# Rotary embedding on one core: the first batch's output stored in four quarters, one of them from SyncE's queue

## The chip, the cores and the metric

The kernel runs on one core of a Trainium2 chip. The metric is the device time of one execution in microseconds (us). The kernel before the change takes 163.11 us, the median of three runs (163.11 to 163.17).

## The reference

The input `x` is 8 batches of 2048 positions, 8 heads and 64 numbers, all float32 (33.5 MB); `cos` and `sin` are tables of 2048 x 32. The output has the size of `x`.

```python
x1 = x[..., :32]
x2 = x[..., 32:]
out1 = x1 * cos - x2 * sin
out2 = x1 * sin + x2 * cos
return concatenate([out1, out2], axis=-1)
```

Every number of `x` is read once and every number of the output is written once.

## The kernel before

**Tiling.** One batch is one tile of 128 partitions. A partition holds R = 16 consecutive positions of 512 numbers each, so a partition's row of a batch is 32 KB, and a batch is 4 MB. Five tiles `xts` (NBUF = 5) are used in turn: batch b lies in tile b % 5, the result is written over the input in place, and it is stored from there. So batch 5 can only be loaded when batch 0 has been stored, batch 6 when batch 1 has, and batch 7 when batch 2 has.

**Loads.** `load(b)` (lines 112 to 125) issues from SyncE's queue (SP). Batch 0 comes in three parts of 4, 4 and 8 positions (rows of 8, 8 and 16 KB in each partition), every other batch in one DMA with rows of 32 KB. Batches 0 to 4 are issued at the start (lines 135 to 137), one behind the other. For b of 5 and more, `load` first waits on SP for all stores of batch b - 5.

**Stores.** `store(b, lo, n, needs)` (lines 127 to 132) stores positions lo to lo + n of batch b. It waits on the issuing engine for the work that makes them. It issues from ScalarE's queue (ACT), except that the last batch is stored from SP. The list `FIRST` (line 269) cuts batch 0 into stores of 4, 4 and 8 positions, `LAST` cuts batch 7 into 7, 5, 3 and 1; the other batches are stored whole.

**Queues in the profile.** DMAs issued by SP are the DMA queue q1, those by ACT are q10. Both run on the same 16 DMA engines. A DMA over 128 partitions gives each DMA engine eight rows.

**Compute.** `PLANS` (lines 259 to 268) splits each batch into pieces. A piece of kind A (`on_vector`) takes one multiply on GpSimd (POOL, line 198, with the swapped halves and the sine), one multiply with the cosine (line 202) and one addition (line 221) on VectorE (DVE). Pieces B and C (`on_tensor`) leave the addition to TensorE (PE, lines 249 and 250), and ScalarE copies the sum back (line 253). Batch 0 is four A pieces of four positions. Its four additions end one after the other, and the loop behind each piece (lines 283 to 289) issues a store as soon as its positions are done. Every engine works in the order in which the loop over the batches emits the instructions.

Of the kernel before, what the change touches and what calls it, by code (L numbers as in the profile page):

```python
# [10 lines left out]
def kernel(  # L11
# [7 lines left out]
    nc = tc.nc  # L19
# [11 lines left out]
    NBUF = 5  # L31
    C = 512
    last = B - 1
# [44 lines left out]
    def wait(engine, point):  # L78
        engine.wait_ge(point[0].sem, point[1])  # L79
        mine = known.setdefault(engine, {})  # L80
        for count, v in [point, *told.get(point, {}).items()]:
            mine[count] = max(v, mine.get(count, 0))
# [10 lines left out]
    def need(engine, *points):  # L93
        for count, v in points:
            if v > known.get(engine, {}).get(count, 0):
                wait(engine, (count, v))
# [15 lines left out]
    def load(b):  # L112
        parts = [(0, 4), (4, 4), (8, 8)] if b == 0 else [(0, R)]
        if b >= NBUF:
            for point in stored[b - NBUF]:
                wait(nc.sync, point)
        for lo, n in parts:
            cols = slice(lo * HD, (lo + n) * HD)
            ins = nc.sync.dma_start(out=xts[b % NBUF][:, cols], in_=xv[b, :, cols])
            point = Count(f"ld{b}_{lo}").by(ins, nc.sync, 16)  # L120
            for r in range(lo, lo + n):
                landed[(b, r)] = point
            if b == 0 and lo == 0:
                cos_in = Count("cos_in").by(nc.sync.dma_start(out=cos_sb, in_=cos_src), nc.sync, 16)
        return cos_in if b == 0 else None

    def store(b, lo, n, needs):
        engine = nc.sync if b == last else nc.scalar
        need(engine, *needs)
        cols = slice(lo * HD, (lo + n) * HD)  # L130
        ins = engine.dma_start(out=ov[b, :, cols], in_=xts[b % NBUF][:, cols])
        stored.setdefault(b, []).append(Count(f"st{b}_{lo}").by(ins, engine, 16))

    sin_in = Count("sin_in").by(nc.scalar.dma_start(out=sin_sb, in_=sin_src), nc.scalar, 16)
    cos_in = load(0)
    for b in range(1, NBUF):
        load(b)

    need(nc.gpsimd, prod.by(nc.gpsimd.memset(eye, 0.0), nc.gpsimd))  # L139
    eye_done = prod.by(  # L140
# [71 lines left out]
    def on_vector(b, lo, n):  # L212

        nonlocal t1_read, turn
        pair = pairs[turn]
        turn = (turn + 1) % len(pairs)
        at, done = sines(b, lo, n, pair, 0)
        need(nc.vector, t1_read, landed[(b, lo)])
        wait(nc.vector, pair.by(times(t1[:, : n * HD], cos_ps, b, lo, n), nc.vector))
        t1_read = dve.by(  # L220
            nc.vector.tensor_add(out=region(b, lo, n), in0=t1[:, : n * HD], in1=products(at, n)),  # L221
            nc.vector,
        )
        read[at : at + n] = [t1_read] * n
        return t1_read

    def on_tensor(b, lo, n, crossed=False):


        nonlocal copied  # L230
        if crossed:
            at, before = place(n, n // 2)
            need(nc.vector, landed[(b, lo)], *before, sin_done)
            need(nc.vector, dve.by(times(products(at, n), sin_ps, b, lo, n), nc.vector))
        else:
            at, made = sines(b, lo, n, prod, n // 2)
            need(nc.vector, made)
        wait(nc.tensor, dve.by(times(region(b, lo, n), cos_ps, b, lo, n), nc.vector))
        xt, prods = region(b, lo, n), products(at, n)
        if crossed:  # L240
            xu, tu = (a.rearrange("p (g u d) -> p g u d", u=2, d=Dh) for a in (xt, prods))
            groups = [slice(j * 2 * H, (j + 1) * 2 * H) for j in range(n // 2)]
            work = [(xu[:, g, u], tu[:, g, 1 - u], eye if u else neye) for g in groups for u in range(2)]
        else:
            cols = [slice(j * HD, (j + 1) * HD) for j in range(n)]
            work = [(xt[:, c], prods[:, c], eye) for c in cols]
        for xj, tj, sign in work:
            wait(nc.tensor, copied)
            nc.tensor.matmul(o, eye, xj, start=True, stop=False)  # L249
            summed = mm.by(nc.tensor.matmul(o, sign, tj, start=False, stop=True), nc.tensor)  # L250
            wait(nc.scalar, summed)
            src = o.rearrange("p (g d) -> p g d", d=Dh) if crossed else o
            copied = act.by(nc.scalar.copy(xj, src), nc.scalar)  # L253
            read[at : at + n] = [summed] * n
        return copied
# [10 lines left out]
        "B1 A5 A5 A5",  # L266
        "B2 A5 A5 A4",
    )
    FIRST = [(0, 4), (4, 4), (8, 8)]
    LAST = [(0, 7), (7, 5), (12, 3), (15, 1)]  # L270
    wait(nc.tensor, eye_done)
    for b in range(B):
        plan, lo = [], 0
        for tile_ in PLANS[b].split():
            plan.append((tile_[0], lo, int(tile_[1])))
            lo += int(tile_[1])
        shares = {0: FIRST, last: LAST}.get(b, [(0, R)])
        done = {}
        for kind, lo, n in plan:
            point = on_vector(b, lo, n) if kind == "A" else on_tensor(b, lo, n, kind == "C")  # L280
            for r in range(lo, lo + n):
                done[r] = point
            while shares and all(r in done for r in range(shares[0][0], sum(shares[0]))):
                s0, sn = shares.pop(0)
                needs = {}
                for r in range(s0, s0 + sn):
                    count, v = done[r]
                    needs[count] = max(v, needs.get(count, 0))
                store(b, s0, sn, needs.items())
        if b + NBUF <= last:  # L290
            load(b + NBUF)
    for b in range(last + 1 - NBUF, last - 1):
# [49 lines left out]
```

## Time and profile before

| | |
|---|---|
| Median of three runs | 163.11 us |
| Time of the profiled execution | 163.16 us |
| Its span, from the first instruction to the last | 161.4 us |
| DVE busy | 140.3 us (87%) |
| POOL busy | 131.1 us (81%) |
| PE busy | 49.8 us (31%) |
| Bytes moved by DMA | 67.66 MB, mean 419 GB/s |
| Last addition on DVE, start and length | 150.91 us, 2.29 us |

The span is 1.8 us shorter than the time of the same execution; these 1.8 us lie before the first and behind the last instruction of the program. All places in time below count from the start of the span. For a queue the profile gives its packets, the bytes, and the time of its packets as a share of the 16 DMA engines' span. The time "to landing" of a DMA runs from its issue to its last semaphore update, so it includes the time in which it stood behind other DMAs.

### The profile page before, as it was taken

To read this page: it belongs to the slowest core of one execution; us is meant where nothing else is said; L and a number is where in the kernel's file an instruction comes from. 1 tells how busy PE (TensorE), PEld (TensorE's weight loads), DVE (VectorE), ACT (ScalarE), POOL (GpSimd) and SP (SyncE) were. 2 spreads that over 40 slices of the span, in tenths; PEclk is the share of its full clock that TensorE was granted. 3 is DMA by queue.
4 is the path that set the end of the run, shared out by engine and by line. 5 is a ranking of instruction groups with operands and counts; after the bars stand their busy time and mean duration, and the time that the engine had idled before them with its cause. 6 is when DMAs were issued, how large, how long until landed. Compare 5 with 4: busy or idle time off the path is not lost.

```text
span 161.4 us, 412 instructions
## 1 busy us (share of the span) xinstructions
PE 49.8 (31%) x76; PEld 16.3 (10%) x76; DVE 140.3 (87%) x55; ACT 14.8 (9%) x25; POOL 131.1 (81%) x35
## 2 busy tenths in 40 slices
PE   0000000048686400068886811830072001840000
PEld 0000000022222100022221301200020001210000
DVE  0069999999999999999999999799999999799900
ACT  3320000001212100001112110110001000110000
POOL 1399996996999989942995599999999999999100
PEclk9999999999999975555579995796555555597555
DMA  5999998998998999999999999999999999998996
GB/s 154 427 455 418 431 487 357 455 487 357 479 431 325 455 496 414 390 496 414 390 496 414 390 496 414 390 496 414 390 496 414 390 496 414 390 487 375 435 406 252
DMA packets 3603, 67.66 MB, mean 419 GB/s; under 512 B 400, under 2 KB 400, under 8 KB 912
## 3 DMA queue, kind: packets, MB, share of 16 engines
q1 hardware_dynamic: 2160, 38.01, 55.5%
q10 hardware_dynamic: 1440, 29.62, 42.7%
q14 instruction: 3, 0.02, 0.0%
HBM read 34.08 MB, written 33.55 MB: 419 GB/s over the span
## 4 chain that ended last, share of the span: by engine, by line
DVE 51%; POOL 35%; issue 5%; DMA 4%; POOLq 0%; ACTq 0%; SPq 0%
POOL t L198 32%; DVE t L202 24%; DVE xt L221 23%; DVE xt L202 5%; DMA sin_sb<-in_sin_dram 4%; POOL t L184 3%; POOLq L79 0%; ACTq L337 0%; SPq L85 0%
## 5 line engine op out<-in xcount | busy, mean ns | idle before, releaser
L198 POOL TENSOR_TENSOR t<-xt,sgn 128x2560 f32<-128x2560 f32 (+3 forms) x27 | 125.8, 4688 | 12.9 <-DVE xt L221 4.5
L202 DVE TENSOR_TENSOR t<-xt,cos_ps 128x2560 f32<-128x2560 f32 (+1 forms) x23 | 61.8, 2687 | 8.3 <-ACT cos_ps L156 7.7
L221 DVE TENSOR_TENSOR xt<-t,t 128x2560 f32<-128x2560 f32 (+1 forms) x23 | 61.8, 2685 | 4.6 <-POOL t L198 2.7
L249 PE MATMUL o<-xt,eye 128*128 128x512 f32 x38 | 27.9, 825 | 93.1 <-DVE xt L202 83.5
L253 ACT COPY xt<-o 128x512 f32<-128x512 f32 x19 | 11.1, 585 | 123.4 <-PE o L250 123.4
L249 PEld LDWEIGHTS o<-xt,eye 128*128 128x128 f32 x38 | 7.1, 233 | 112.8 <-DVE xt L202 53.1
L250 PE MATMUL o<-t,eye 128*128 128x512 f32 x26 | 16.5, 722 | 0.0
L202 DVE TENSOR_TENSOR xt<-xt,cos_ps 128x512 f32<-128x512 f32 (+2 forms) x7 | 11.2, 1594 | 0.1
L250 PE MATMUL o<-t,neye 128*128 128x512 f32 x12 | 8.8, 826 | 0.0
L250 PEld LDWEIGHTS o<-t,eye 128*128 128x128 f32 x26 | 6.1, 235 | 8.4 <-issue 8.4
L202 DVE TENSOR_TENSOR t<-xt,sin_ps 128x3072 f32<-128x3072 f32 x2 | 6.7, 3344 | 0.0
L184 POOL TENSOR_TENSOR t<-xt,sin_sb 128x1024 f32<-128x1024 f32 x1 | 2.3, 2347 | 5.0 <-DMA sin_sb<-in_sin_dram 5.0
L250 PEld LDWEIGHTS o<-t,neye 128*128 128x128 f32 x12 | 3.2, 264 | 4.5 <-issue 4.5
L184 POOL TENSOR_TENSOR t<-xt,sgn 128x1024 f32<-128x1024 f32 x1 | 2.3, 2323 | 0.0
L153 ACT ACT_TABLE_LOAD x1 | 1.3, 1283 | 1.3 <-SPq L85 1.3
L153 ACT ACTIVATE sgn<-sin_sb 128x512 f32<-128x512 f32 x1 | 0.6, 629 | 4.0 <-DMA sin_sb<-in_sin_dram 4.0
L139 POOL MEMSET eye<- 128x128 f32 x1 | 0.2, 204 | 0.5 <-SPq L85 0.5
L157 ACT COPY sgn<-sin_sb 128x512 f32<-128x512 f32 x1 | 0.6, 608 | 0.0
L156 ACT COPY cos_ps<-cos_sb 128x512 f32<-128x512 f32 x1 | 0.6, 580 | 0.0
L158 ACT COPY sin_ps<-sin_sb 128x512 f32<-128x512 f32 x1 | 0.6, 580 | 0.0
L141 POOL TENSOR_SCALAR_AFFINE_SELECT eye<-eye 128x128 f32<-128x128 f32 x1 | 0.3, 293 | 0.2 <-POOL eye L139 0.2
L161 ACT ACTIVATE neye<-eye 128x128 f32<-128x128 f32 x1 | 0.3, 307 | 0.0
(4 smaller groups left out, 0.4 us busy)
## 6 DMA issues: line engine op xcount, KB each, us to landing
xt<-in_x_dram SPq DMA_DIRECT2D x7, 4096.0 KB, 33.9
out_dram<-xt ACTq DMA_DIRECT2D x6, 4096.0 KB, 23.4
xt<-in_x_dram SPq DMA_DIRECT2D x2, 1024.0 KB, 6.5
xt<-in_x_dram SPq DMA_DIRECT2D x1, 2048.0 KB, 12.1
out_dram<-xt ACTq DMA_DIRECT2D x2, 1024.0 KB, 19.0
out_dram<-xt ACTq DMA_DIRECT2D x1, 2048.0 KB, 28.5
out_dram<-xt SPq DMA_DIRECT2D x1, 1792.0 KB, 11.4
out_dram<-xt SPq DMA_DIRECT2D x1, 1280.0 KB, 9.4
```

What stands on the lines that cost most here:

```text
L141: nc.gpsimd.affine_select(out=eye, in_=eye, compare_op=mybir.AluOpType.not_equal, fill=1.0, base=0, pattern=[[-1, P]], channel_multiplier=1,),
L153: nsin_done = act.by(nc.scalar.mul(sgn[:, :, 0, :], sin_sb, -1.0), nc.scalar)
L156: cos_done = act.by(nc.scalar.copy(cos_ps, cos_sb), nc.scalar)
L157: sgn_done = act.by(nc.scalar.copy(sgn[:, :, 1, :], sin_sb), nc.scalar)
L158: sin_done = act.by(nc.scalar.copy(sin_ps, sin_sb), nc.scalar)
L184: nc.gpsimd.tensor_mul(out=tu[:, :, u, :].rearrange("p (r h) d -> p r h d", h=H), in0=xu[:, :, 1 - u, :].rearrange("p (r h) d -> p r h d", ...
L198: ins = nc.gpsimd.tensor_mul(out=out, in0=swapped, in1=repeat(sgn[:, lo : lo + n], H))
L202: return nc.vector.tensor_mul(out=out.rearrange("p (r k d) -> p r k d", r=n, d=Dh), in0=region(b, lo, n).rearrange("p (r k d) -> p r k d", ...
L221: nc.vector.tensor_add(out=region(b, lo, n), in0=t1[:, : n * HD], in1=products(at, n)),
L249: nc.tensor.matmul(o, eye, xj, start=True, stop=False)
L250: summed = mm.by(nc.tensor.matmul(o, sign, tj, start=False, stop=True), nc.tensor)
L253: copied = act.by(nc.scalar.copy(xj, src), nc.scalar)
```

## The change

Batch 0 is stored in four DMAs of four positions each, all with rows of 8 KB, where before there were two of 8 KB rows and one of 16 KB rows. The second of the four (positions 4 to 7) is issued from SP and not from ACT. The loads of batches 3 and 4 are no longer issued at the start: they are issued on SP right behind this store, so SP's queue holds the loads of batches 0, 1 and 2, then the store, then the loads of batches 3 and 4. What the other engines run, and in which order, is as before.

```diff
     def store(b, lo, n, needs):
-        engine = nc.sync if b == last else nc.scalar
+        engine = nc.sync if b == last or (b, lo) == (0, 4) else nc.scalar
...
     cos_in = load(0)
-    for b in range(1, NBUF):
-        load(b)
+    load(1)
+    load(2)
...
-    FIRST = [(0, 4), (4, 4), (8, 8)]
+    FIRST = [(0, 4), (4, 4), (8, 4), (12, 4)]
...
                 store(b, s0, sn, needs.items())
+                if (b, s0) == (0, 4):
+                    load(3)
+                    load(4)
```

## The prediction

> **What bounds the kernel now.** I read the page's slices and its queues first. In the slices of about 4 us the digits of DVE and of the DMA engines are 8 or 9 nearly throughout, so there are two candidates.
>
> ```profile
> DVE  0069999999999999999999999799999999799900
> ...
> DMA  5999998998998999999999999999999999998996
> ...
> q1 hardware_dynamic: 2160, 38.01, 55.5%
> q10 hardware_dynamic: 1440, 29.62, 42.7%
> ```
>
> The queues' shares add up to 98.2% of 161.4 us, or 158.5 us of work on each of the 16 DMA engines. The trace's packet records show all 16 occupied from 2.5 to 159.8 us with no gap. Next I looked at the end: the timeline of the last stores and the last addition.
>
> ```profile
> 143.56 10.76 SPq L131 DMA_DIRECT2D out_dram<-xt  x4
> ...
> 150.91 2.29 DVE L221 TENSOR_TENSOR xt<-t,t 128x2048 f32<-128x2048 f32 x1
> ```
>
> DVE's last addition ends at 153.20 us and the last store is issued at 153.60, but the landings run on to 160.5 us. What DVE releases last is 768 + 256 KB, which at the queues' 432 GB/s is 2.4 us. The other 4 us or so are stores that were released earlier and still stand in line. The chain of waits names DVE and POOL because it follows semaphores; it does not see a DMA standing behind another. So the DMA engines set the end, and compute has a few microseconds of slack there. The time can only change if the DMA engines get more or less work, if they run dry somewhere, or if compute slips by more than its slack.
>
> **How the queues share an engine.** These are issues and landings of single DMAs: the load of batch 2 (issued 3.38), the load of batch 4 (4.40) and the second store of batch 0 (18.35).
>
> ```profile
> xt<-in_x_dram SPq DMA_DIRECT2D x1, 4096.0 KB, 34.7
> ```
>
> ```profile
> xt<-in_x_dram SPq DMA_DIRECT2D x1, 4096.0 KB, 66.3
> ```
>
> ```profile
> out_dram<-xt ACTq DMA_DIRECT2D x1, 1024.0 KB, 22.7
> ```
>
> The loads run in the order of issue: batch 2 lands at 38.1 us, batch 3 at 52.5, batch 4 at 70.7. The store of 1 MB lands at 41.1 us, so it takes 12 us from the first store's landing (29.0). In the packet records each engine alternates between the queues row by row: 1.213 us for a load row of 32 KB, 0.309 us for a store row of 8 KB. Eight such pairs are 12.2 us, as seen. A store row of 16 KB takes 0.611 us.
>
> **Part 1, smaller rows.** The half with 128 rows of 16 KB becomes 256 rows of 8 KB: 2 x 0.309 - 0.611 = 0.007 us for each, times eight rows per engine, is +0.06 us. One more DMA adds one completion packet of 0.009 us per engine. Does a DMA more cost anything besides? Not where DMAs queue: the last two stores (768 and 256 KB, issued one behind the other) land 0.65 us apart, no more than the 0.67 us of eight rows of 2 KB (0.084 us each).
>
> **Part 2, SP waits for DVE.** SP now holds the loads of batches 3 and 4 until the second addition ends, at 18.3 us instead of 4. Two issues at about 0.5 us each make it 19.4. Until 37.7 us the queue still has the loads of batches 1 and 2, so the cover is 18 us and the cost nothing. Without that cover the queue would stand empty and the store queue alone could not fill the engines. Nothing else waits in SP at that time: the load of batch 5 waits for the stores of batch 0, which now land earlier. ACT issues three DMAs as before, the last of them again at about 27.7 us.
>
> **Part 3, the order of rows.** Up to 37.7 us nothing moves: ACT's queue still has 8 KB rows, now those of the third store (issued at 23.0) in the place of the second. At 37.7 us ten store rows of 8 KB are left in q10 (two of the third, eight of the fourth) and the eight of the second store are next in q1. They alternate 8 KB by 8 KB: 16 x 0.309 = 4.9 us without a load row. So the load of batch 3 starts at about 42.6 us and lands at 53.2 to 53.8 us instead of 52.5. All stores of batch 0 are done at about 45 us, where before they ended at 56.1. From then to the first row of batch 1's store (issued at 52.08) the loads have the engines to themselves. The load of batch 4 lands 0.1 us later if that store's first rows come as late as before (about 56 us), and up to 1.8 us later if they start at once. Who waits for it:
>
> ```profile
> 70.73 1.27 POOL L198 TENSOR_TENSOR t<-xt,sgn 128x512 f32<-128x512 f32 x1 [1.80 <-DMA xt<-in_x_dram]
> 75.56 11.35 POOL L198 TENSOR_TENSOR t<-xt,sgn 128x2560 f32<-128x2560 f32 x2 [3.57 <-DVE xt L221]
> ```
>
> POOL waits for batch 4's load already, but behind its 1.27 us piece it waits 3.57 us for DVE. A delay up to 3.5 us ends in that wait. Later loads shift likewise by 0.1 to 1.8 us. Batch 7's lands at 128.75 now, and POOL comes to it at 132.0 (the chain of waits has a step of POOL there): 3.3 us of slack. Where loads are later, stores are earlier by the same bytes; once all loads are in (131 us at the latest) the queues hold what they held before. Cost: nothing, as long as the engines are never idle, and I find no place where both queues are empty.
>
> **Part 4, a stall.** The windows over the time of the 16 KB rows show one stretch that is slower than its neighbour.
>
> ```profile
> 41.60:48.90 7.30, 5.82 (x12) 1.90 (x12) 7.27 (x4) 1.26 (x3) 7.19 (x2) 1.00 1.00 431
> 48.90:51.30 2.40, 1.85 (x4) 0.68 (x4) 2.37 (x2) 0.49 (x1) 2.40 (x1) 1.00 1.03 382
> ```
>
> The last two columns are the DMA share and GB/s. In the second window the engines are as busy but move 382 GB/s. In the packet records the load rows begun at 49.7 us take 1.50 to 1.68 us on all 16 engines, which adds 0.35 us; those at 40.5 us add 0.10 us, those between 15 and 24 us 0.11 us. I find no such thing behind 50 us, where rows of 32 KB meet rows of 32 KB. The pairing of 32 KB loads with 16 KB store rows is gone after the change, but why the rows stall I can't tell. The gain has a bound of 0.45 us (the two after 38 us); the loss, if the new pairing of 8 KB with 8 KB stalls once in the same way, of 0.35 us. I take half of the gain, -0.2 us.
>
> **Part 5, a store between loads in one queue.** Each engine turns from loads to stores and back inside q1. No row of before shows this. From below it is nothing: it alternates between a load row and a store row all the time between the queues, at 431 GB/s and a share of 1.00. From above, the first load rows of 8 KB at the start, with no work ahead to hide their latency, took 0.6 to 0.95 us instead of 0.309: some 0.55 us more, twice 1.1 us. I take nothing, since q10 has rows at both turns, as in the nearer row. The Trainium skill (Perfetto Trace Analysis, DMA Optimizations) advises one engine for inputs and another for outputs, which speaks against this part; no store stands ahead of a load in one queue here, so this trace can't show it.
>
> **Sum.** 163.16 + 0.07 - 0.2 = 163.03 us for an execution like the profiled one, which lies 0.05 us above the median of the runs; so 163.0 us. I count what is within 0.2% (0.33 us) as no change, about what a measurement of this kernel can tell.
>
> **The rivals.**
> - All stalls from 15 us on go away: -0.56 + 0.07, about 162.65 us. For it: they only come where rows of unequal size share the engines, and that time shrinks from 40 to 30 us. Against: those before 24 us arise in a stretch that the change leaves alone. Losing the two after 38 us alone gives 162.75, just outside no change. Chance 0.27.
> - Slower by the turns in q1, at 37.7 and 42.6 us: if the first load row behind the stores isn't fetched ahead, each turn stands open up to 0.55 us, so 163.5 to 164.3 us. It decides from 0.4 us in sum. For it: nothing in this trace hides a cold load row but a row of the other queue, and a row of 8 KB hides only 0.309 us. Against: the same engines switch direction at each row now. Chance 0.24, in which I include that such a stall as at 49.7 us comes twice in the new order.
> - A fixed cost for the added DMA. The first store was issued at 13.70 us into an empty queue, and the packet records show its first row at 17.35, 3.6 us later. If the new store cost this with the other queue empty as well, the time would be 166.8 us. It stands behind 18 us of loads with q10 full beside it: chance 0.01. The Trainium skill (DMA: Bandwidth & Descriptors, Rules for kernel authors, with the cost in Anatomy of one DMA) speaks for this rival: coalesce small transfers, as each DMA has a fixed cost of about 2 us; by that figure the estimate would be some 165 us. On the two last stores, as said, the trace disagrees.
> - Batch 4 so late that POOL and then DVE slip: needs over 3.5 us at POOL and another 2 us of slack at the end. By part 3 at most 1.8 us, so its chance is 0.02 and I leave it inside no change.
> - The change doesn't do what it says: if the second store held up the loads, batch 3 would land far behind 54 us; the order on SP and the 18 us of cover speak against it (0.01, with the slower cases).
>
> **How the numbers follow.** No change has 0.47: the DMA engines' work is the same within 0.07 us, and the rest is stalls of a few tenths. Faster 0.27; slower 0.24 + 0.01 + 0.01 = 0.26. The range goes from 162.5 (all stalls gone, and a little of the median's difference) to 164.0 (most of the turns' price); I leave out some 2 in 10, above all in the upper end. The likeliest case alone spans 162.8 to 163.4 us.
>
> **What would show it.** Right: the shares of q1 and q10 still add up to about 158 us, q1 with more packets and q10 with as many as before; the second store lands at about 43 us and batch 5's load is issued near 45 to 46 us instead of 56.2; POOL still waits for DVE behind its short piece of batch 4; DVE's last addition ends within 1 us of 153.2. The stall is settled by the windows between 38 and 56 us: under 430 GB/s at a full share means stalled rows. Wrong: a DMA share under 1 around 38 or 43 us (the turns), a POOL wait of several microseconds for batch 4 or 7, or a last addition later than 156 us.

## Result and the profile after: slower by 0.8%

The changed kernel takes 164.49 us, the median of 18 runs (163.13 to 165.50); the kernel before, beside it on the same chip, 163.11 us (18 runs, 163.02 to 163.99). The ratio is 1.008 with a 95% interval of 1.0056 to 1.0104. I had forecast no change, 163.0 us with a range of 162.5 to 164.0. The changed kernel also varies by 2.4 us from run to run, where the kernel before, one run apart, stays within 0.4 us. The profiled execution took 163.90 us, so it is one of the quicker ones; its span is 162.1 us. (All ratios compare executions that lie within 1.5% of the fastest of their kernel, which leaves out the profiled one of run 6 below, 168.49 us; a ratio isn't the quotient of the two medians.)

Page of the kernel after, slices and queues (packets, MB, share of 16 engines):

```profile
DVE  0179999999999999999999999999999999699500
...
DMA  5999898997998998999998999999999999999995
...
q1 hardware_dynamic: 2304, 39.06, 56.8%
q10 hardware_dynamic: 1440, 28.57, 41.3%
```

The queues' shares add up to 98.1% of 162.1 us, 159.0 us per engine where before it was 158.5. The bytes are the same, q1 has 144 packets more (the second store's 128 and its completions) and q10 as many as before. So some 0.5 us of the 0.74 us by which this execution is longer is time in which rows took longer, not idle time.

Timeline of the kernel after (start, busy time, engine and line, instruction; idle time before it and its releaser in brackets):

```profile
72.23 1.27 POOL L198 TENSOR_TENSOR t<-xt,sgn 128x512 f32<-128x512 f32 x1 [3.62 <-DMA xt<-in_x_dram]
75.24 11.34 POOL L198 TENSOR_TENSOR t<-xt,sgn 128x2560 f32<-128x2560 f32 x2 [1.74 <-DVE xt L221]
...
143.57 10.21 SPq L131 DMA_DIRECT2D out_dram<-xt  x4
149.88 2.29 DVE L221 TENSOR_TENSOR xt<-t,t 128x2048 f32<-128x2048 f32 x1
```

Compute isn't late. POOL waits 1.82 us longer for batch 4's load and 1.83 us shorter for DVE behind it. The last addition ends at 152.17 us, 1.03 us earlier than before, and the last store is issued 1.03 us earlier (152.57 for 153.60). Yet it lands 0.75 us later, at 161.27. That is 8.7 us from issue to landing in the place of 6.9. The DMA engines have to be looked at, and by stretches.

Windows (length; busy time of PE, PEld, DVE, ACT and POOL; PE's clock, DMA share, GB/s). The kernel before:

```profile
68.00:80.00 12.00, 8.71 (x10) 2.98 (x11) 11.90 (x5) 1.17 (x2) 6.63 (x3) 0.50 1.01 437
93.00:99.00 6.00, 0.33 (x1) 0.00 (x0) 5.61 (x3) 0.58 (x1) 6.00 (x3) 0.78 1.01 437
157.00:160.00 3.00, 0.00 (x0) 0.00 (x0) 0.00 (x0) 0.00 (x0) 0.00 (x0) 0.50 0.89 363
160.00:161.30 1.30, 0.00 (x0) 0.00 (x0) 0.00 (x0) 0.00 (x0) 0.00 (x0) 0.50 0.06 19
```

The kernel after:

```profile
35.90:37.60 1.70, 1.70 (x3) 0.34 (x1) 1.67 (x2) 0.00 (x0) 1.52 (x1) 1.00 1.00 361
...
68.00:80.00 12.00, 9.03 (x12) 3.03 (x12) 11.90 (x5) 1.17 (x2) 6.64 (x3) 0.56 1.01 434
93.00:99.00 6.00, 0.00 (x0) 0.00 (x0) 5.96 (x3) 0.00 (x0) 6.00 (x3) 0.72 1.02 431
...
157.00:160.00 3.00, 0.00 (x0) 0.00 (x0) 0.00 (x0) 0.00 (x0) 0.00 (x0) 0.50 0.95 391
160.00:161.30 1.30, 0.00 (x0) 0.00 (x0) 0.00 (x0) 0.00 (x0) 0.00 (x0) 0.50 0.20 77
```

(A share a little above 1 is a full one: the records of rows reach over the window's edge.) In the stretches where loads and stores of 32 KB rows run together the share stays full, but the rate is 434 and 431 GB/s where before it was 437. In the first window, beside the 8 KB stores, it is 361: the last load row of batch 2, begun at 36.0 us, takes 0.27 us longer than usual on the mean of the 16 engines. Run 14's profile below, of 163.18 us, has it too (0.28 us), so it isn't what sets them apart. At the end the engines are still moving 77 GB/s from 160.0 us on, where before there was almost nothing left.

The packet records in the trace resolve this into two numbers. The first is the **stall**: what load rows of 32 KB and the other rows take above their usual time (1.213 us for 32 KB), summed and divided by 16 engines, from 14 us on. The second is the **spread**: the time between the first and the last of the 16 DMA engines to finish the same DMA. Neither is a line of the page; both are worked out from the records of single rows.

| profiled execution | time | stall | of it behind 56 us | spread, last store | middle engine done | slowest done |
|---|---|---|---|---|---|---|
| before | 163.16 | 0.60 | 0.02 | 0.46 | 160.13 | 160.52 |
| after | 163.90 | 1.01 | 0.55 | 1.06 | 160.49 | 161.27 |

The slowest engine is done 0.75 us later: 0.36 us because all are later, and 0.39 us because the slowest lies further behind the middle one. In the kernel before the spread is 0.26 to 0.32 us for every DMA up to 141 us, so the 16 engines work in step. In the kernel after it is 0.35 to 0.51 us for most DMAs up to 54 us, 0.71 at the second store, 0.74 at batch 4's load, 0.42 again at the next three DMAs (to 93.7 us), and mostly 1.0 to 1.1 us from batch 6's load (111 us) on, with single DMAs at 0.78 and 1.64. The stalls behind 56 us are of a kind that the kernel before has nowhere: around 71, 90.5 and 110 us on the last row of a store, around 73.6, 93.2 and 112.8 us on the load row ahead of the next store's first row, each on 7 to 9 of the 16 engines only and by up to 0.55 us. Smaller ones follow in the middle of a batch, mostly at 117 to 120 us (up to 0.15 us).

What is different ahead of them? ACT's queue runs empty. The last rows of batch 0 end between 45.6 and 46.1 us, and batch 1's store is issued at 51.72; its first rows come at 55.3, 3.6 us behind the issue. In the kernel before that store, issued at 52.08, follows directly behind batch 0's rows, on all 16 engines at 56.7 to 57.0 us. So in the changed kernel a queue starts up anew in the middle of the work. In this execution the engines take it up together, within 0.51 us (55.29 to 55.80), so the restart itself doesn't put them out of step here. The order is another as well: batch 1's store lands 2.1 us behind batch 4's load (74.26 and 72.17), where before it was 4.8 us (75.45 and 70.66). In the packet records one row of the store is left when a load ends, where before there were two. What the experiments had to tell apart: the store between the loads in SP's queue (Q in the expectations), the smaller rows of the quarters (S), the emptied queue and its restart (R), the other order of rows (P, the distance of the streams of loads and stores), and engines out of step, whatever brings it about (R in its sharper form).

### The profile page after: what moved, and what is told of

It reads as the page before. It is cut to its first block, busy times and chain, and to the rows that moved or that the text cites. A ratio compares the mean times of both kernels' runs of the same rounds, so it can differ in the third digit from the quotient of the medians.

```text
span 162.1 us, 414 instructions
## 1 busy us (share of the span) xinstructions
PE 51.7 (32%) x76; PEld 16.8 (10%) x76; DVE 140.4 (87%) x55; ACT 14.9 (9%) x25; POOL 131.1 (81%) x35
## 4 chain that ended last, share of the span: by engine, by line
DMA 45%; DVE 40%; POOL 8%; issue 1%; SPq 0%; POOLq 0%; ACTq 0%
DMA xt<-in_x_dram 26%; DVE xt L221 19%; DMA out_dram<-xt 19%; DVE t L202 18%; POOL t L198 5%; POOL t L184 3%; DVE xt L202 2%; SPq L340 0%; POOLq L79 0%; ACTq L79 0%; SPq L85 0%; POOLq L300 0%
## 5 line engine op out<-in xcount | busy, mean ns | idle before, releaser
L249 PE MATMUL o<-xt,eye 128*128 128x512 f32 x38 | 28.9, 851 | 91.2 <-DVE xt L202 81.6
L250 PE MATMUL o<-t,eye 128*128 128x512 f32 x26 | 18.4, 801 | 0.0
L250 PE MATMUL o<-t,neye 128*128 128x512 f32 x12 | 7.9, 745 | 0.0
L250 PEld LDWEIGHTS o<-t,eye 128*128 128x128 f32 x26 | 6.7, 258 | 9.5 <-issue 9.5
```

## Experiments

Ratios are to the kernel before, run beside each on the same chip (its medians: 163.1 to 163.2 us).

**1. The quarters alone.** All four from ACT, the loads at the start as before.

```diff
-    FIRST = [(0, 4), (4, 4), (8, 8)]
+    FIRST = [(0, 4), (4, 4), (8, 4), (12, 4)]
```

> Batch 0 in four quarters of 8 KB rows, all four from ACT, all five loads issued at the start as before the change. Theory P (what matters is how many rows the stream of loads is ahead of the stream of stores once both move 32 KB rows: 2 rows before the change, 1 row after it; at 1 row some rows stall where a batch begins or ends, and the 16 DMA engines drift apart): the store of batch 1 begins some 10 us later here, the distance is several rows, and the time is within 0.3 us of 163.1 with landings of one DMA spread over some 0.3 us. Theory Q (the store that stands between loads in one queue puts the engines out of step, and they stay so): there is none here, 163.1 to 163.2 us. Theory S (rows of 8 KB instead of 16 KB cost the time): 164 us or more.

Measured: 164.11 us, 1.0055 (1.0043 to 1.0067). So it is slow without any store among the loads. But one thing I had not planned: with 8 KB rows in ACT's queue the loads get four fifths of the bytes for longer, batch 4 lands at 62.9 us (before 70.7), batch 0's last store only at 63.55, and the load of batch 5 is issued at 63.6. Here it is SP's queue that runs empty. The 16 engines finish batch 1's store 2.56 us apart, and the rate falls. Windows of this kernel:

```profile
77.00:79.00 2.00, 1.57 (x4) 0.38 (x2) 1.97 (x2) 0.39 (x1) 2.00 (x1) 1.00 1.08 328
68.00:80.00 12.00, 8.26 (x14) 3.02 (x15) 11.90 (x5) 1.76 (x3) 7.70 (x3) 0.80 0.97 396
```

396 GB/s over 12 us where before it was 437, and 328 in the worst two.

**2. The move alone.** Stores of 4, 4 and 8 positions as before, the second from SP between the loads.

```diff
-        engine = nc.sync if b == last else nc.scalar
+        engine = nc.sync if b == last or (b, lo) == (0, 4) else nc.scalar
...
+                if (b, s0) == (0, 4):
+                    load(3)
+                    load(4)
```

> Batch 0 in 4, 4 and 8 positions as before the change, but the second store from SP between the loads of batches 2 and 3. Theory Q: as slow as the changed kernel, 164 to 165 us, spread of the landings over 0.6 us from the second store on. Theory S: 163.1 us, as the 16 KB rows are back. Theory P: the distance of the two streams decides; worked out from the rows it is 1 or 2 (the load of batch 2 lands about 1.5 us later, so the loads are later than in the changed kernel, and the stores end at about the same time): at 2 rows 163.1 to 163.4 us, at 1 row 164 to 165 us.

Measured: 164.12 us, 1.0042 (1.0011 to 1.0073). So it is slow without the quarters too. The last rows in its q10 end at 42.4 us, and its profile (163.90) has nearly the numbers of the changed kernel: stall 1.03 (0.52 behind 56 us, at the same places), spread mostly 1.0 to 1.1 us from batch 7's load on, where until batch 4's load it was 0.3 to 0.9. Here too the engines take up batch 1's store together (55.36 to 55.80 us). Neither half is the whole cause by itself; what both share is that a queue runs empty and that the order of rows behind it changes.

**3 and 4. Moving the order of rows: two edits that fell short.** Four copies ahead of the issue of batch 1's store were to delay it in the changed kernel (3) and in the kernel before, there with a tiny load of 16 partitions behind the loads (4).

```diff
+        if b == 1:
+            for j in range(4):
+                nc.scalar.copy(pad[:, j, :], eye)
```

> The changed kernel, and ScalarE makes four copies of a 128x128 tile into scratch space, each of some 0.3 us, between its wait for batch 1 and the issue of batch 1's store, so that this store starts about one load row (1.2 us) later and the loads are 2 rows ahead as before the change. Theory P: the time returns to within 0.3 us of 163.1, the landings spread over 0.3 to 0.5 us, no stalled rows behind 70 us. Theories Q and S: nothing changes, 164 to 165 us.

> The kernel before the change with two additions: behind the load of batch 4 a tiny load of 16 partitions x 128 B (one row and one completion packet for each DMA engine, each a turn in which a store row goes ahead), and the same four scratch copies of ScalarE ahead of batch 1's store. The first takes two rows off the distance of the streams, the second adds one: 1 row as in the changed kernel, with no quarter and no store among the loads. Theory P: 164 to 165 us and varying from run to run, stalled rows near 71, 91 and 110 us. Theories Q and S: 163.1 to 163.3 us.

Measured: 164.81 us, 1.0079 (1.0052 to 1.0106), and 163.32 us, 1.001 (0.9997 to 1.0024). The copies didn't delay anything: the store was issued at 51.91 us while they ran (51.90 to 52.80). So run 3 is in effect the changed kernel again, and run 4 the kernel before with one tiny row more per engine in q1, which shifts the order by a row and costs nothing that can be told. In run 4's profile (163.12) two of the 16 engines take their load rows a turn apart from the others around 106 us, so that batch 6's load lands 1.57 us apart, and behind 56 us all rows together stall for 0.04 us: engines at different turns need not cost anything. The profile of run 3 (164.87) shows the start of the emptied queue at its worst: the first rows of batch 1's store come at 55.41 to 55.98 us on eleven engines and at 57.54 to 57.74 on the other five, one load row later. A window of this kernel later on:

```profile
93.00:99.00 6.00, 0.15 (x1) 0.00 (x0) 5.65 (x3) 0.59 (x1) 6.00 (x3) 0.77 0.97 366
```

366 GB/s where before it was 437; the stall is 2.04 us, more than three times that of before.

**5 to 8. Empty queues by themselves.** Run 5: the changed kernel with its last quarter as two DMAs of 4 KB rows, so that ACT's queue lasts longer. Run 6: the kernel before with 16 copies ahead of batch 1's store, each waited for, so that its queue has a gap as the changed kernel's has. Run 7: the changed kernel with four such waited copies. Run 8: the kernel before with the load of batch 5 issued only when DVE is at about 70 us, so that SP's queue is without rows for some 5 us (in its profile from 69 to 73.6).

```diff
-    FIRST = [(0, 4), (4, 4), (8, 4), (12, 4)]
+    FIRST = [(0, 4), (4, 4), (8, 4), (12, 2), (14, 2)]
```

```diff
+        for _ in range(16 if b == 1 else 0):
+            wait(nc.scalar, act.by(nc.scalar.copy(pad, eye), nc.scalar))
```

```diff
+            if b == 3 and kind == "C":
+                wait(nc.sync, (dve, dve.n))
+                load(5)
+                load(6)
```

> The changed kernel with the last quarter of batch 0 stored as two DMAs of 4 KB rows, so that ACT's queue still has rows (until about 58 us) when batch 1's store is issued at 51.7; in the changed kernel it is empty from 46.5 us to about 54. Theory R (a queue that runs empty and starts again is picked up by the 16 DMA engines at different turns; from then on rows stall, the engines drift apart, and the slowest sets the end): 163.1 to 163.5 us with little variation, hardly a stalled row behind 56 us. Theory Q (the store among the loads does it): 164 to 165.5 us and varying. Theory S (small rows): as slow as the changed kernel or slower, by 0.15 us for 256 more packets.

> The kernel before the change, but ScalarE makes 16 copies of 128x128, each waiting for the one ahead, between its wait for batch 1 and the issue of batch 1's store, so that this is issued near 58 us and not at 52: ACT's queue is empty from 56 us for 3 to 4 us. Loads, rows and queues are as before the change. Theory R: 163.6 to 165 us, varying from run to run, stalled rows behind 56 us. Theories Q and S: 163.1 to 163.3 us.

> The changed kernel with four such copies, each waiting for the one ahead (about 1.5 us), ahead of the issue of batch 1's store: the loads come 2 rows ahead of the stores as before the change, but ACT's queue still runs empty. Theory P (the distance of the streams): within 0.3 us of 163.1. Theory R: as the changed kernel, 163.4 to 165.5 us from run to run.

> The kernel before the change, but the load of batch 5 waits besides for the cosine product of batch 3's first piece (about 70 us), so that SP's queue runs empty for some 2 us at 70.5 us, behind the load of batch 4. Theory R: 163.6 to 165 us, varying, stalled rows behind 72 us and the landings of one DMA spread over 1 us or more. Theories Q, S and P with a distance still over one row: 163.1 to 163.5 us.

| run | median | ratio |
|---|---|---|
| 5, changed, queue just filled | 163.48 | 1.0036 (1.0019 to 1.0054) |
| 6, before, gap in q10 | 163.63 | 1.0043 (1.002 to 1.0067) |
| 7, changed, store 1 later | 163.75 | 1.0041 (1.002 to 1.0062) |
| 8, before, gap in q1 | 163.50 | 1.002 (1.0011 to 1.0029) |

Runs 6 and 8 are the plain ones: no quarters, no moved store, the same rows, and yet slower by 0.43% and 0.2%. In run 6 ACT's later copies are held up as well, by some 7 us; I have not read from a profile that this is harmless, so run 8 is the cleaner of the two. In its profile two of the 16 engines take up batch 5's load one turn behind the others. Runs 5 and 7 gain back about half. In run 5 the queue is filled only just: its rows last until 55.5 to 55.9 us and the store is issued at 53.5, but its first rows come at 58.0 to 58.4. In its profile (163.25) that gap of some 2 us did no harm: all engines start within 0.4 us, and behind 56 us the rows stall for 0.05 us. In run 7 the queue still runs empty and only the place of the start is another; there (163.49) twelve engines take the store up at 56.5 to 56.9 us and four at 58.1 to 58.5.

**9 to 11. Order and step, without an empty queue.** Run 9 gives the kernel before the order of the changed one (batch 1's store landing 2.2 us behind the last load ahead of batch 5's, where the changed kernel has 2.1) by tiny DMAs in both queues, 32 partitions on SP and 16 on ACT. Run 10 adds to the kernel before one tiny load on 8 partitions behind the loads, so that half of the DMA engines have extra turns in q1 and the others none. Run 11 is run 1 with the load of batch 5 in two parts, the first of which is issued in time to keep SP's queue filled.

```diff
+    extra = [Count("tiny").by(nc.sync.dma_start(out=pad[:8, :Dh], in_=cos[:8, :]), nc.sync, 16)]
```

> The kernel before the change with two tiny DMAs into scratch space that nobody waits for until the end: on SP behind the load of batch 4, 32 partitions x 128 B (two rows and a completion packet per DMA engine, three turns), and on ACT ahead of batch 1's store, 16 partitions x 128 B (two turns). The distance of the streams becomes 2 - 3 + 2 = 1 row as in the changed kernel, and no queue runs empty. Theory P (a distance of one row stalls rows): 163.9 us or more, stalls of some 0.5 us per engine between 56 and 130 us. Theory R (a queue that ran empty and restarts): 163.1 to 163.4 us, hardly a stall.

> The kernel before the change with one tiny load on SP behind batch 4's, over 8 partitions only, so it may run on 8 of the 16 DMA engines: those take two turns more, and then half of the engines are two rows apart from the others in what they alternate, with no queue running empty. Theory R in its sharper form (what hurts is that engines no longer take load and store rows at the same turns, whatever brings it about): 163.5 to 165 us, varying, with stalls. Theory R in its plain form (only the restart hurts) and theory P (distances 0 and 2, both harmless): 163.1 to 163.4 us.

> Batch 0 in four quarters, all from ACT, all loads at the start (as in the run with the split alone, 164.1 us), but batch 5's load cut into positions 0 to 6 and 7 to 15, and the first part waits only for the first two stores: SP's queue has rows when batch 4's load ends at 63 us, where it ran empty before. Theory R: back to 163.1 to 163.5 us. Theory S (8 KB rows): still 164 us. Theory P: the distance of the streams stays many rows, so this run and the one without the cut should be alike.

Measured: run 9 163.95 us, 1.0042 (1.0023 to 1.0061); run 10 164.21 us, 1.0059 (1.0046 to 1.0072); run 11 163.82 us, 1.0046 (1.0027 to 1.0064). Run 10 is the clearest result of the study. It adds 1 KB of transfer, and the engines' usual work is that of before; behind batch 4's load they are only put out of step. (In the profiled executions of runs 8 and 10 batch 1's store was issued at 53.8 us, and ACT's queue misses one turn of 1.2 us ahead of it, on all engines alike; SP's queue in run 10 goes on without a gap.) Batch 1's store then lands 2.78 us apart on the 16 engines, the stall behind 56 us is 1.76 us where it was 0.02, and the windows show it (this kernel, the stretch of before's 437 GB/s):

```profile
68.00:80.00 12.00, 8.15 (x13) 2.82 (x14) 11.90 (x5) 1.75 (x3) 7.73 (x3) 0.75 0.99 388
```

Run 9 says that an order one row apart costs something even without a gap: its spread grows from 0.4 to 0.8 us at 111 to 130 us, with stalls of 0.21 us behind 56 us. In its packet records the rows around 90 and 110 us follow each other as in the first profile of the changed kernel, and the rows that stall are the same: the last row of a store (90.6, 110.0 us), the load row ahead of the next store (93.3, 112.4 to 112.8) and some at 117 to 120 us. So the pattern of that profile doesn't need an empty queue. Run 11 settles nothing, as its rows of 14 KB bring a stall of their own (0.44 us at 63.7 us).

**12 to 16. Filling the emptied queue, and another order in step.** Run 12 is the changed kernel unaltered. Run 13 adds to it one tiny DMA of 128 partitions in ACT's queue behind the last quarter, which gives each engine eight tiny rows there; each takes a turn against a load row of 32 KB and so holds the queue open. Run 14 adds another of 32 partitions. Run 15 adds one of 16 partitions at that place to the kernel before, run 16 a tiny load of 32 partitions behind its loads.

```diff
+                if (b, s0) == (0, 12):
+                    ins = nc.scalar.dma_start(out=pad[:128, :Dh], in_=sin[:128, :])
+                    extra.append(Count("fill0").by(ins, nc.scalar, 16))
```

> The changed kernel once more, for a second profile of the same instructions. Theory R: between 163.1 and 165.5 us from run to run; the profiled run's time goes with how far the 16 engines' last landings of a DMA lie apart and with the stalls. If the stalls and the spread are as in the first profile while the time differs by over 0.5 us, theory R does not carry the variation.

> The changed kernel with one tiny DMA on ACT behind the last quarter of batch 0: 128 partitions x 128 B into scratch space, eight rows and a completion packet per DMA engine, each taking a turn beside a load row, so that ACT's queue has rows until about 57 us, when batch 1's store has been issued. The loads are then some 4 rows ahead of the stores. If the empty queue and the one-row distance that follows from it are what the change costs, 163.2 to 163.5 us with nearly all runs under 163.7. If the store among the loads or the quarters cost it, 164 to 165.5 us as the changed kernel.

> As the one before, with a second tiny DMA of 32 partitions behind the first (three turns more): the queue has rows until some 60 us, and the distance is one to two rows more. Same expectations: 163.2 to 163.5 us if the empty queue is the cause; 164 to 165.5 us if not. If the first of the two is fast and this one is slow, the distance decides and not the empty queue.

> The kernel before the change with one tiny DMA on ACT (16 partitions, two turns) ahead of batch 1's store: no queue runs empty, the loads are 4 to 5 rows ahead in place of 2 to 3. If only a distance of one row or engines out of step hurt: 163.1 to 163.4 us. If each change of the order away from the one before the change hurts: 163.5 us or more, varying.

> The kernel before the change with one tiny load on SP behind batch 4's (32 partitions, three turns): no queue runs empty, and the stores come about one row ahead of the loads, or level with them. If a distance of about one row hurts on either side: 163.6 us or more, varying, with stalls at the ends of batches. If only the loads one row ahead hurt: 163.1 to 163.4 us.

| run | median | ratio | profiled | its stall (behind 56 us) | its spread, last store |
|---|---|---|---|---|---|
| 12, changed | 164.50 | 1.006 (1.0041 to 1.008) | 164.01 | 1.00 (0.56) | 1.04 |
| 13, changed, filler | 163.66 | 1.0038 (1.002 to 1.0057) | 164.43 | 1.00 (0.08) | 1.25 |
| 14, changed, two fillers | 163.40 | 1.0022 (1.0002 to 1.0042) | 163.18 | 0.56 (0.08) | 0.45 |
| 15, before, other order | 163.15 | 0.9996 (0.9987 to 1.0005) | 163.03 | 0.51 (0.02) | 0.47 |
| 16, before, other order | 163.42 | 1.0022 (1.0005 to 1.004) | 163.73 | 1.13 (0.43) | 0.66 |

With two fillers the changed kernel, quarters, moved store and all, is back within 0.22% of the kernel before. Its profiled execution takes 163.18 us and looks like before's by every number in the table, and there batch 1's store begins on all engines within 0.4 us (60.32 to 60.70) behind tiny rows that end at 59.1 to 59.5. It isn't the whole loss in the median. Its interval lies clear of the changed kernel's first one (1.0056 to 1.0104), but it overlaps run 13's and just touches run 12's. Nor does it keep the order: batch 1's store lands 12 us behind batch 4's load there, so run 14 undoes the empty queue and the one-row order together and can't tell them apart. Run 15 moves the order of rows by more than the change does (batch 1's store lands 9.6 us behind batch 4's load, where before it was 4.8 and in the changed kernel 2.1), with no gap and the engines in step, and costs nothing. Windows of run 15:

```profile
68.00:80.00 12.00, 8.37 (x15) 3.07 (x16) 11.90 (x5) 1.76 (x3) 6.58 (x3) 0.81 1.01 437
```

437 GB/s, as before. The profiled executions of runs 12 and 13 also show something that the first profile of the changed kernel doesn't. Between 42.5 and 43.6 us, where q1 turns from the second store to batch 3's load, eight store rows stall by 0.06 to 0.30 us, and so do first load rows behind the turn: in run 12 mostly by up to 0.2 us but on two engines by 0.55 and 0.68, in run 13 on three engines by 0.18 to 0.29. That is 0.24 and 0.14 us on the mean, and the spread at batch 3's landing is 0.81 and 0.85 us where it was 0.48. So the engines can fall out of step at the turn as well, in some executions. In run 13, whose ACT queue doesn't run empty, the spread is 1.25 us by batch 4's landing and 1.25 at the last store; the load row between the tiny rows and batch 1's store takes 0.45 to 0.69 us longer on fifteen engines there (at 55.4 to 55.8 us) and 0.93 on the last.

Run 12's stall has the size of the first profile's (1.00 for 1.01, 0.56 for 0.55 behind 56 us), but it lies elsewhere: 0.54 us of it at 57.8 to 59.6 us, on the load row ahead of batch 1's first store row, on all 16 engines, and next to nothing at the ends of later batches. One engine takes the store up at 61.29 us and the others at 59.4 to 60.5. So two executions of the same kernel lose nearly the same time in different places. (They differ by 0.11 us, so the test by 0.5 us that the expectation names didn't come about.)

**17 and 18. Fillers for runs 2 and 1.** The move alone with the two fillers on ACT, and the quarters alone with a tiny load of 64 partitions on SP, were to show whether either half is free once its queue stays filled.

> The second store on SP between the loads, batch 0 in 4, 4 and 8 positions (no quarters of the second half), and the two tiny DMAs (128 and 32 partitions) on ACT behind the third store, so that ACT's queue has rows until some 58 us: the store among the loads alone, without an empty queue. If the turn from stores to loads in SP's queue adds to the loss: 163.4 to 164.5 us, varying, with rows stalled near 43 us in the slow runs. If only the empty queue does: 163.1 to 163.4 us.

> The four quarters alone, all from ACT and all loads at the start (164.1 us before), with one tiny load of 64 partitions on SP behind batch 4's (five turns), so that SP's queue has rows from 63 us until batch 5's load comes: the quarters without an empty queue. If the empty queue made the 164.1: 163.1 to 163.5 us, the landings of batch 1's store no longer 2.6 us apart. If the quarters did: 164 us.

Measured: 165.40 us, 1.014 (1.0118 to 1.0163), and 163.94 us, 1.0047 (1.0023 to 1.007). Both missed their aim. In run 17 the fillers had landed at 47.7 and 51.4 us, and the store was issued at 53.6; in run 18 the first row of batch 5's load came at 67.35 us, some 2 us behind the tiny load's last packet. The queues still ran empty, so neither tells the halves apart. Run 17 is the slowest of all; in its profiled execution (163.65) one engine takes up batch 1's store a turn ahead of the others (57.01 us, the others 58.25 to 58.53), so that batch 4's load lands 1.65 us apart (0.57 in run 2), and why the fillers made it worse I can't tell. No version beat the kernel before; run 15 equals it.

## Why the prediction was wrong

**What held.** Part 1: the usual time of all rows together is 157.35 us per engine for 157.29 before, +0.06 as worked out. Part 2: SP's wait cost nothing; the second store was issued at 18.03 us, and the loads of batches 3 and 4 stood in the queue long before their turn. The order of part 3 came as drawn: batch 3 landed at 53.73 us (forecast 53.2 to 53.8), batch 4 1.5 us later than before (0.1 to 1.8), the second store at 43.80 (about 43), batch 5's load was issued at 46.55 (45 to 46, so a little late). Batch 7 was 2.15 us later, a little past the 1.8, and POOL waited 1.04 us for it. The last addition ended within the microsecond. Single DMAs of the kernel after, second store and load of batch 4 (us to landing last):

```profile
out_dram<-xt SPq DMA_DIRECT2D x1, 1024.0 KB, 25.8
...
xt<-in_x_dram SPq DMA_DIRECT2D x1, 4096.0 KB, 53.3
```

Compute, and the idea that the DMA engines set the end, were right.

**The step that failed is the price at the end of part 3**: "Cost: nothing, as long as the engines are never idle". The engines were never idle, as forecast. I had written down that all of batch 0 would be stored at about 45 us and that the loads would then have the engines to themselves, so the empty q10 was in the prediction, and I priced it and the new order of rows at zero because a saturated engine has no use for a second queue. Runs 6 and 8 price such a gap at 0.33 to 0.7 us by themselves (0.2% and 0.43% of 163.1), and run 9 prices the one-row order without a gap at 0.7 us (0.42%). What I hadn't considered is what comes behind the gap. In some executions the engines take the queue up at different turns (5 of 16 a turn late in run 3, 4 in run 7, 1 in run 12). In the first profile they took it up together, and the stalls came at the ends of batches in the new order.

**Part 4 looked at the wrong stretch.** The two stalls after 38 us did go (-0.45 us), but the last load row of batch 2 took 0.27 us longer in their place, and the rows between 14 and 25 us 0.08 more: 0.46 us up to 56 us for 0.58, so -0.12 of the -0.2 that I took. Behind 56 us, with 32 KB against 32 KB, the changed kernel has 0.55 us for 0.02. I had taken these rows to be free of stalls, because the kernel before shows none there. In all it is 1.01 us for 0.60, so +0.41 where I took -0.2.

**The sum took 16 engines for one.** All terms were means over engines. The end is set by the slowest, and that term, 0.39 us of the 0.75, had no place in the sum. The working with it: +0.06 (rows), +0.41 (stalls), -0.11 (the middle engine's remaining difference to 0.36, not explained further), +0.39 (slowest behind the middle) = +0.75 us, from 160.52 to 161.27.

**The rivals.** The turns in q1 (163.5 to 164.3) came nearest by the price, with the double stall that I had put into it. The first profile has no slow row and no share under 1 between 38 and 43 us. Its slow load row at 36.0 us stands right ahead of the first turn, but the kernel before has the like on batch 3's last row (49.7 us, 0.35), where q1 doesn't turn, so it can't be put down to the turn. Runs 12 and 13 do have stalls at the second turn, in run 12 with the full price on two engines (0.55 and 0.68 us on the first load row behind the stores). So this rival is a part of the loss in some executions; how large a part in the median is open. The fixed cost of an added DMA (166.8) is out. Yet the 3.6 us that it used, from an issue into an empty queue to the first row, came true at another place: at batch 1's store, where it isn't lost as such (loads fill the time). The 2 us of the Trainium skill that I set beside it (DMA: Bandwidth & Descriptors, Anatomy of one DMA) are a fit for DMAs issued by GpSimd, and the rule (Rules for kernel authors) speaks of transfers under 64 KB; the stores here are of 1 MB, from SP and ACT. On the page that I cited for one engine for inputs and another for outputs, the Trainium skill (Perfetto Trace Analysis, DMA Optimizations): run 2, which moves only the store, is slower by 0.42%, so it isn't contradicted; but an emptied queue goes with the move, and run 2 can't show which of the two it was.

**What is shown, and what is open.** Shown: engines out of step can be enough for a loss of this size (run 10), though they need not cost anything (run 4's profile); an emptied queue alone is enough for a part of it (runs 6 and 8); an order one row apart is, with no gap (run 9), but another order need not cost anything (run 15); and filling the queue, which also moves the order, brings most of the loss back (run 14). Not shown: which of these makes the changed kernel's loss. A restart at different turns can't be it in the first profile, where all 16 engines took the store up within 0.51 us. That the variation by 2.4 us comes from where each execution's engines take up the queue is argued only (that store was issued at 51.72 us in one profile of the changed kernel and at 55.52 in the other). Open: the shares of the restart, of the one-row order and of the turn at 42.6 us; and why a load row stalls beside the first row of a store. The Trainium skill (DMA: Bandwidth & Descriptors, in its table of latencies and other measured facts, the row on HBM row pitch) has a measured loss of rate for rows a large power of two apart, and infers from it that streams in lock-step collide in the memory's channels. No run here changed addresses, so nothing here tests it.

## What to carry to other kernels

Where the DMA engines bound the kernel, a full DMA share isn't enough: look at each queue for the time at which it runs empty, at the first rows behind it on every engine, and at the order in which loads and stores end from there on. Sum the work up to the slowest engine, not the mean one, and read the spread of one DMA's landings over the engines as a number of its own. A change that moves no bytes can still put engines out of step that were in step, and then also look at how much the time varies, since one profiled run may be a lucky one, and two of the same kernel can lose their time in different places.

## What I had not expected of the hardware

- A DMA that is issued into an empty queue shows its first row some 3.6 us later (13.70 to 17.35 us in the kernel before, 51.72 to 55.3 in the kernel after, 69.79 to 73.6 in run 8), also while the other queue keeps the engine full.
- Engines take turns by rows, whatever the size: a tiny row or a completion packet (0.009 us) uses up a turn like a row of 32 KB (1.213 us). One tiny load on 8 partitions cost 0.59% this way (run 10).
- Engines out of step come back only in part: in the kernel after the spread is 1.0 to 1.1 us for most DMAs from 111 us to the end, and in run 1 it falls from 2.56 us to 0.87, no further.
- ScalarE issues a DMA while earlier copies of its own still run (issue at 51.91 us, copies from 51.90 to 52.80, run 3).
